# Decoder layer in float32r pairs: one list of weight splits for the whole layer, and VectorE's transposes tied behind it

## The chip, the core and the metric

One core of a Trainium2 chip (trn2) runs one launch. The metric is the device time of an execution in microseconds (us). The engines named below are TensorE (PE in the profile, with PEld for its weight loads), VectorE (DVE), ScalarE (ACT), GpSimd (POOL) and SyncE (SP), which issues most DMAs.

## The reference, cut to what matters

One decoder layer on 256 tokens, 2048 channels, everything in float32:

```
h    = rmsnorm(x);  proj = h @ w_in          # 2048 x 13312: glu, q, k, v, q_xa, three gates
conv = conformer(glu) ; da = diff_attention(q, k, v) ; xa = cross_attention(q_xa, rmsnorm(mem) @ w_mem_kv)
merged = g0 * (conv @ w_conv_out) + g1 * (da @ w_da_out) + g2 * (xa @ w_xa_out)
x = x + merged @ w_mix_out
x = x + square(relu(rmsnorm(x) @ w_up)) @ w_down      # 2048 -> 8192 -> 2048
return rmsnorm(x)
```

The products with the weights are nearly all of the work, and each weight is used once.

## The kernel before

**How a product is made.** float32 is split into two float32r parts: hi, a rounded copy, and lo, the rest. A product is then three matmuls: hi x whi, hi x wlo, lo x whi. `group` (L297) makes one block of 512 columns for all 256 tokens: over k in steps of two k tiles (a *block*, 256 rows of a weight), it loads raw (512 KB, SyncE's queue, L319), lets ScalarE write whi (L327) and VectorE wlo = raw - whi (L328), and runs 12 matmuls (2 k tiles, 2 token tiles, 3 products, L309 to L311) into two PSUM banks. A group over 2048 rows has eight blocks, over 1024 rows four. There are 560 blocks. Tiles rotate: raw has 5 buffers, whi 4, wlo 3. After the last block, `evac` hands the result on.

**The groups in order.** w_in for the convolution (4 groups), w_mem_kv (4), w_in for q_xa, q, k, v (8). Then, four times, three gate groups (w_in) and one group each of w_xa_out, w_da_out, w_conv_out, whose gated sum is a chunk `mg`. Then four groups of w_mix_out, whose results are added to x (tiles x1, L892). Then four times (j): four groups of w_up, each giving a chunk `ru`, and four of w_down (L933 adds to x1).

**Transposes.** The stationary operand of a product must be an activation with features on the partitions. Chunks mg, x1 and ru have tokens there, so `to_parts_dve` (L265) turns a chunk of 512 features with VectorE's 32 x 32 transposes: `block_transpose2` (L253, for mg, ru, and also kx and xq) takes 16 instructions of 32x256, `block_transpose` (L241, for x1, which lies in one tile for each token tile) 32 instructions of 32x128. Then two conversions follow, each of hi by ScalarE and of lo by VectorE (L272 to L284).

**What sets the order.** Such work is a generator in a `Task` (L78), put in a lane by `spawn` (L128). After each block of matmuls `side_step` (L137) ticks the task at the head of each lane: one step up to its next `yield`, at rate 1. A group whose activation is not finished calls `finish` on its task before the matmuls that need it (L333). So a chunk's task is spread over the blocks of the next group in the program. [...] `later` (L143) adds an edge of order alone: the first instruction is not put before the second.

Of the kernel before, what the change touches and what calls it, by code (L numbers as in the profile page):

```python
# [10 lines left out]
F32 = mybir.dt.float32  # L11
F32R = mybir.dt.float32r
I32 = mybir.dt.int32
U32 = mybir.dt.uint32
AF = mybir.ActivationFunctionType
# [4 lines left out]
P = 128  # L20
# [12 lines left out]
WARM = 8  # L33
LAMBDA_INIT = 0.8 - 0.6
# [4 lines left out]
def _turn_pieces(n):  # L39
    """1/(2 pi) cut into n float32 pieces of 12 bits each."""  # L40
    digits = "0.15915494309189533576888376337251436203445964574045644874766734405889679763"
    from fractions import Fraction

    rest = Fraction(digits)
    out = []
    for i in range(n):
        ulp = Fraction(1, 2 ** (14 + 12 * i))
        q = rest // ulp
        out.append(float(q * ulp))
        rest -= q * ulp  # L50
    return out


class Act:
    """An activation, transposed: [feature, token] as two float32r parts whose sum is the float32 value."""
# [22 lines left out]
class Task:  # L78
    def __init__(self, gen, rate=1.0):
        self.gen = gen  # L80
        self.rate = rate
        self.credit = 0.0
        self.done = False
# [20 lines left out]
def decoder_layer_kernel(  # L104
# [18 lines left out]
    # ---------------------------------------------------------------- side work  # L123
# [4 lines left out]
    def spawn(gen, lane="t", rate=1.0):  # L128
        t = Task(gen, rate)
        lanes[lane].append(t)  # L130
        return t
# [11 lines left out]
    def later(ins, first):  # L143
        """Keeps work that nothing else holds back from being issued before `first`."""
        tc.add_manual_dep(
            ins.ins, first.ins.name,
            mybir.DependencyInfo(mybir.DependencyClass.NoSync, mybir.DependencyReason.DATA),
            reason="issue order",
        )
# [6 lines left out]
    # ---------------------------------------------------------------- constants  # L156
# [3 lines left out]
    with tc.high_priority():  # L160
        nc.vector.memset(neg_half, -0.5)
        nc.vector.memset(ones, 1.0 / CH)
        make_identity(nc, ident)
        # the tensor engine's clock rises only under load
        pw = psum.tile([P, P], F32, tag="at", name="pw")
        for _ in range(WARM):
            nc.tensor.matmul(pw, ones, ones, start=True, stop=True)
        warm = const.tile([P, 1], F32, name="warm")
        nc.scalar.activation(warm, neg_half[:, 0:1], AF.Square)
# [26 lines left out]
    # ---------------------------------------------------------------- pieces  # L196
    def rsqrt_of(ss, n, dim, name):
        """(ss / dim + eps) ** -0.5 for a [P, n] of sums of squares."""
        m = const.tile([P, n], F32, name=name + "_m")
        nc.vector.tensor_scalar(m, ss, 1.0 / dim, EPS, ALU.mult, ALU.add)  # L200
        rv = const.tile([P, n], F32, name=name)
        nc.gpsimd.tensor_tensor(rv, m, neg_half[:, :n], op=ALU.pow)
        return rv
# [14 lines left out]
    def to_parts(src, dst, kt0, nkt, gname=None):  # L218
        """src [tok, NT, nkt * P] -> the transposed parts of dst from k tile kt0."""
        for b in range(0, nkt, 2):  # L220
            ps = psum.tile([P, 2, S], F32, tag="tr", name="tr")
            for c in range(2):
                for t in range(NT):
                    transpose(ps[:, c, t * P : (t + 1) * P], src[t][:, (b + c) * P : (b + c + 1) * P])
            yield
            k = kt0 + b
            if gname is None:
                nc.scalar.copy(dst.hi(k, 2), ps)
                nc.vector.tensor_tensor(dst.lo(k, 2), ps, dst.hi(k, 2).bitcast(F32), op=ALU.subtract)
            else:  # L230
                for c in range(2):
                    g = vcol(gname, k + c)
                    nc.scalar.activation(dst.hi(k + c), ps[:, c : c + 1, :], AF.Copy, scale=g)  # L233
                for c in range(2):
                    g = vcol(gname, k + c)
                    nc.vector.scalar_tensor_tensor(
                        dst.lo(k + c), ps[:, c : c + 1, :], g, dst.hi(k + c).bitcast(F32), ALU.mult, ALU.subtract
                    )
            yield

    def block_transpose(src, dst):  # L241
        """src, one [tok, G] for each token tile -> dst [feature, G // P, tok], by 32 x 32 blocks on the vector engine."""
        B = 32
        for q in range(P // B):
            for c in range(P // B):
                for t in range(NT):
                    nc.vector.transpose(  # L247
                        dst[c * B : (c + 1) * B, :, t * P + q * B : t * P + (q + 1) * B],
                        src[t].rearrange("p (j c k) -> p j c k", c=P // B, k=B)[q * B : (q + 1) * B, :, c, :],
                    )  # L250
            yield

    def block_transpose2(src, dst):  # L253
        """As block_transpose, of one [tok, NT, G] tile."""
# [3 lines left out]
        for q in range(P // B):  # L258
            for c in range(P // B):
                nc.vector.transpose(  # L260
                    out_v[c * B : (c + 1) * B, :, :, q * B : (q + 1) * B], in_v[q * B : (q + 1) * B, :, :, c, :]
                )
            yield

    def to_parts_dve(src, dst, kt0, gname=None):  # L265
        """src [tok, NT, G], or a list by token tile -> the transposed parts of dst from k tile kt0."""
        st = work.tile([P, G // P, S], F32, tag="chunk", name="st", bufs=4)
        yield from (block_transpose if isinstance(src, list) else block_transpose2)(src, st)
# [17 lines left out]
    def transpose_plain(src, dst, kt0, nkt):  # L286
        """src [tok, NT, nkt * P] -> dst [feature, kt, tok], float32."""
# [8 lines left out]

    def group(w, r0, c0, act, evac, prep=None, split=0):  # L297
        """psum[t] = act^T [tok, K] @ w[r0 : r0 + K, c0 : c0 + G], each handed to evac(t, psum).

        The last `split` blocks of k run token tile by token tile."""  # L300
# [12 lines left out]
        held = []  # L313
        for kb in range(nkb):
            k = kb * KB
            if prep is not None:
                prep(k)
            raw = wpool.tile([P, KB, G], F32, tag="raw", name="raw", bufs=5)
            ld = nc.sync.dma_start(  # L319
                raw, w[r0 + k * P : r0 + (k + KB) * P, c0 : c0 + G].rearrange("(c p) n -> p c n", p=P)  # L320
            )
            if prep is not None and kb < 2:
                later(ld, first_load[kb])
            whi = wpool.tile([P, KB, G], F32R, tag="whi", name="whi", bufs=4)
            wlo = wpool.tile([P, KB, G], F32R, tag="wlo", name="wlo")
            with tc.high_priority():
                nc.scalar.copy(whi, raw)  # L327
                nc.vector.tensor_tensor(wlo, raw, whi.bitcast(F32), op=ALU.subtract)  # L328
# [39 lines left out]
    # ---------------------------------------------------------------- normed x  # L368
# [17 lines left out]
    # rotary tables, taps, lambda  # L386
# [69 lines left out]
    # ---------------------------------------------------------------- convolution branch  # L456
# [137 lines left out]
    # ---------------------------------------------------------------- memory: keys and values  # L594
# [26 lines left out]
    # ---------------------------------------------------------------- cross attention  # L621
# [67 lines left out]
    # ---------------------------------------------------------------- differential attention  # L689
# [140 lines left out]
    # ---------------------------------------------------------------- gated merge  # L830
# [12 lines left out]
    def products(c):  # L843
# [14 lines left out]
        tk = spawn(to_parts_dve(mg, mT, c * 4))  # L858
# [7 lines left out]
    # ---------------------------------------------------------------- output projection, residual  # L866
    x1 = [units.tile([P, D], F32, tag="unit", name=f"x1_{t}") for t in range(NT)]
    for t in range(NT):
        later(nc.gpsimd.dma_start(x1[t], x[t * P : (t + 1) * P, :]), mark[0])
# [6 lines left out]
    def squares(src, dst, c):  # L876
        for t in range(NT):
            junk = work.tile([P, G], F32, tag="t2k", name="junk", bufs=4)
            nc.scalar.activation(junk, src[t][:, c * G : (c + 1) * G], AF.Square, accum_out=dst[:, t, c : c + 1])

    def x1_task(c):
        yield from to_parts_dve([x1[t][:, c * G : (c + 1) * G] for t in range(NT)], x1T, c * 4, "g_mlp")
        squares(x1, ss1, c)
# [4 lines left out]
    for c in range(NC4):  # L888
        def f(ps, c=c):
            for t in range(NT):  # L890
                xs = x1[t][:, c * G : (c + 1) * G]
                nc.vector.tensor_tensor(xs, ps[t], xs, op=ALU.add)  # L892
            tk = spawn(x1_task(c))
# [3 lines left out]
    # ---------------------------------------------------------------- feed forward  # L897
    ss2 = const.tile([P, NT, 8], F32, name="ss2")

    def final_scale(t):  # L900
# [3 lines left out]
        for c in range(NC4):  # L904
            xs = x1[t][:, c * G : (c + 1) * G]
# [8 lines left out]
    for j in range(DFF // D):  # L914
        uu = Act(units, f"ff{j}", 16)
        for g in range(4):
            def f(ps, g=g, uu=uu):
# [5 lines left out]
                tk = spawn(to_parts_dve(ru, uu, g * 4))  # L923
                uu.tasks[g * 4 : g * 4 + 4] = [tk] * 4
            group(w_up, 0, j * D + g * G, x1T, both(f))
        for c in range(NC4):
# [3 lines left out]
            def f(t, ps, c=c, last=last):  # L930
                xs = x1[t][:, c * G : (c + 1) * G]
# [42 lines left out]
```

## Time and profile before

| | |
|---|---|
| measured, median of 3 runs | 1622.68 us (1622.25 to 1623.86) |
| profiled execution, span from first to last instruction | 1620.9 us (the profile gives no time of that execution beyond its span) |
| TensorE busy | 1585.9 us, 98% |
| VectorE busy | 1135.4 us, 70% |
| ScalarE busy | 782.5 us, 48% |
| DMA | 304.79 MB, mean 188 GB/s |
| chain of waits that ended last | TensorE 84%, VectorE 13% |

How to read it: the kernel is one stream of matmuls with short interruptions. A busy share is a mean over all stages. Where TensorE is idle, the rows of its waits say what it waited for, and the order of VectorE's and ScalarE's instructions around that moment says why it came late.

### The profile page before, as it was taken

The page shows a single profiled execution, that of the slowest core. Times are in us where ns is not written, and L with a number is a line of the kernel's source. Part 1 is how long each engine was busy: PE and PEld are TensorE (multiplying, and loading weights), DVE is VectorE, ACT ScalarE, POOL GpSimd, SP SyncE. Part 2 cuts the span into 40 slices and gives each one's busy share as a digit, 9 for nine tenths or more (in the row PEclk, how much of TensorE's full clock was granted, in tenths as well). Part 3 has the DMA queues.
Part 4 walks back from the last instruction along what each step waited for, and adds up shares of the span by engine and source line. Part 5 has one row for each costly group of instructions (what it writes and reads, how often), then busy time and mean ns, then how long its engine had stood idle before and what let it go on. Part 6 is the DMA issues. An engine that isn't in the chain of part 4 may idle for free.

```text
span 1620.9 us, 19587 instructions
## 1 busy us (share of the span) xinstructions
PE 1585.9 (98%) x7020; PEld 1301.2 (80%) x7020; DVE 1135.4 (70%) x1705; ACT 782.5 (48%) x1006; POOL 20.5 (1%) x33
## 2 busy tenths in 40 slices
PE   8999999999999999999999999999999999999997
PEld 7888788888888888888877787887888878887786
DVE  5589989888877456474689877457765676548754
ACT  6554444455784444444344544335543454344543
POOL 1000000010000000000000000000000000000000
PEclk9999999999999999999999999999999999999999
DMA  8665665556556666667655565665656656665563
GB/s 265 199 220 163 193 187 171 160 157 192 158 170 188 199 190 191 194 191 219 239 183 168 170 207 182 195 194 160 203 192 197 183 166 208 194 193 179 167 211 125
DMA packets 156934, 304.79 MB, mean 188 GB/s; under 512 B 9578, under 2 KB 10164, under 8 KB 156452
## 3 DMA queue, kind: packets, MB, share of 16 engines
q1 hardware_dynamic: 156036, 299.96, 60.3%
q0 software_dynamic: 768, 3.57, 0.7%
q8 instruction: 55, 0.90, 0.2%
q14 instruction: 43, 0.35, 0.1%
q10 hardware_dynamic: 32, 0.01, 0.0%
HBM read 301.40 MB, written 2.10 MB: 187 GB/s over the span
## 4 chain that ended last, share of the span: by engine, by line
PE 84%; DVE 13%; issue 2%; DMA 0%; DVEq 0%; ACT 0%; SPq 0%; POOLq 0%; POOL 0%
PE acc L310 28%; PE acc L311 27%; PE acc L309 27%; DVE st L260 6%; DVE wlo L328 4%; DVE st L247 2%; PE tr L173 1%; PE xs L642 0%; PE xo L675 0%; DMA raw<-in_w_in_dram 0%; PE ds L737 0%; DVE kxT L260 0%; PE do L788 0%; DVE conv L487 0%; DVEq L328 0%
## 5 line engine op out<-in xcount | busy, mean ns | idle before, releaser
L328 DVE TENSOR_TENSOR wlo<-raw,whi 128x1024 fp32r<-128x1024 f32 x560 | 682.4, 1224 | 402.8 <-PE acc L310 341.6
L327 ACT CAST whi<-raw 128x1024 fp32r<-128x1024 f32 x560 | 591.1, 1056 | 707.3 <-PE acc L311 671.9
L310 PE MATMUL acc<-wlo,xT_hi 128*128 128x512 f32 x768 | 302.2, 394 | 1.5 <-DVE wlo L328 1.5
L311 PE MATMUL acc<-whi,xT_lo 128*128 128x512 f32 x768 | 299.6, 393 | 0.0
L309 PE MATMUL acc<-whi,xT_hi 128*128 128x512 f32 x768 | 294.0, 395 | 3.0 <-ACT xT_hi L233 3.0
L310 PE MATMUL acc<-wlo,x1T_hi 128*128 128x512 f32 x512 | 200.7, 392 | 11.8 <-DVE wlo L328 11.7
L310 PE MATMUL acc<-wlo,ff_hi 128*128 128x512 f32 x512 | 199.7, 390 | 3.5 <-DVE wlo L328 3.5
L311 PE MATMUL acc<-whi,ff_lo 128*128 128x512 f32 x512 | 199.3, 389 | 0.0
L311 PE MATMUL acc<-whi,x1T_lo 128*128 128x512 f32 x512 | 199.2, 390 | 0.0
L309 PE MATMUL acc<-whi,ff_hi 128*128 128x512 f32 x512 | 193.2, 389 | 0.0
L309 PE MATMUL acc<-whi,x1T_hi 128*128 128x512 f32 x512 | 186.2, 389 | 0.0
L310 PEld LDWEIGHTS acc<-wlo,xT_hi 128*128 128x128 f32 x768 | 144.6, 189 | 32.9 <-DVE wlo L328 3.5
L309 PEld LDWEIGHTS acc<-whi,xT_hi 128*128 128x128 f32 x768 | 144.3, 189 | 32.8 <-ACT xT_hi L233 3.2
L311 PEld LDWEIGHTS acc<-whi,xT_lo 128*128 128x128 f32 x768 | 144.7, 189 | 29.9
L310 PEld LDWEIGHTS acc<-wlo,x1T_hi 128*128 128x128 f32 x512 | 96.1, 188 | 37.5 <-DVE wlo L328 17.7
L310 PEld LDWEIGHTS acc<-wlo,ff_hi 128*128 128x128 f32 x512 | 96.1, 188 | 25.2 <-DVE wlo L328 5.2
L260 DVE STREAM_TRANSPOSE st<-ru 32x256 f32<-32x256 f32 x256 | 111.4, 435 | 3.3
L309 PEld LDWEIGHTS acc<-whi,x1T_hi 128*128 128x128 f32 x512 | 96.1, 188 | 20.1
L309 PEld LDWEIGHTS acc<-whi,ff_hi 128*128 128x128 f32 x512 | 96.1, 188 | 19.9
L311 PEld LDWEIGHTS acc<-whi,ff_lo 128*128 128x128 f32 x512 | 96.1, 188 | 19.8
L311 PEld LDWEIGHTS acc<-whi,x1T_lo 128*128 128x128 f32 x512 | 96.1, 188 | 19.6
L487 DVE SCALAR_TENSOR_TENSOR conv<-uT,taps,conv 128x255 f32<-128x255 f32 (+29 forms) x240 | 98.2, 468 | 0.1
(208 smaller groups left out, 1400.2 us busy)
## 6 DMA issues: line engine op xcount, KB each, us to landing
raw<-in_w_in_dram SPq DMA_DIRECT2D x192, 512.0 KB, 4.3
raw<-in_w_up_dram SPq DMA_DIRECT2D x128, 512.0 KB, 3.9
raw<-in_w_down_dram SPq DMA_DIRECT2D x128, 512.0 KB, 4.8
raw<-in_w_mem_kv_dram SPq DMA_DIRECT2D x32, 512.0 KB, 4.1
raw<-in_w_mix_out_dram SPq DMA_DIRECT2D x32, 512.0 KB, 4.5
raw<-in_w_xa_out_dram SPq DMA_DIRECT2D x16, 512.0 KB, 4.2
raw<-in_w_da_out_dram SPq DMA_DIRECT2D x16, 512.0 KB, 4.7
raw<-in_w_conv_out_dram SPq DMA_DIRECT2D x16, 512.0 KB, 4.6
```

Source lines behind the costliest of these rows:

```text
L173: nc.tensor.transpose(dst, src, ident[:k, :k])
L247: nc.vector.transpose(dst[c * B : (c + 1) * B, :, t * P + q * B : t * P + (q + 1) * B], src[t].rearrange("p (j c k) -> p j c k", c=P // B, ...
L260: nc.vector.transpose(out_v[c * B : (c + 1) * B, :, :, q * B : (q + 1) * B], in_v[q * B : (q + 1) * B, :, :, c, :])
L309: nc.tensor.matmul(ps[t], hi[:, tt], whi[:, c, :], start=kt == 0, stop=False)
L310: nc.tensor.matmul(ps[t], hi[:, tt], wlo[:, c, :], start=False, stop=False)
L311: return nc.tensor.matmul(ps[t], lo[:, tt], whi[:, c, :], start=False, stop=kt == nkt - 1)
L327: nc.scalar.copy(whi, raw)
L328: nc.vector.tensor_tensor(wlo, raw, whi.bitcast(F32), op=ALU.subtract)
L487: ins = nc.vector.scalar_tensor_tensor(conv[:, cb, d:], uT[:, cb, : S - d], w, conv[:, cb, d:], ALU.mult, ALU.add)
```

## The change

- All blocks of all groups stand in one list in the program's order (`plan_groups`). `produce` takes the next one: raw's DMA, whi, wlo. `group` calls it up to twice in a block while at most AHEAD = 3 splits are ready, and takes the oldest. So a split is issued three blocks ahead, across group boundaries. The first group, with its own loads of x, takes them one by one.
- wlo has 4 buffers for 3, raw 4 for 5; whi stays at 4.
- `lo_mark` is the newest wlo issued. Each instruction of `block_transpose2` gets an edge of order behind it. As a step of the task issues four transposes, they lie in fours behind successive wlo.
- `hold`: the tasks of mg, x1 and ru skip their first tick.
- x1 changes from two tiles [P, 2048], one for each token tile, to two tiles [P, 2, NT, 512], so that a chunk of 512 columns has both token tiles side by side. `block_transpose` goes; x1 uses `block_transpose2`. The load of x becomes four DMAs for two.
- Comments and docstrings go.

```
-    def __init__(self, gen, rate=1.0):
+    def __init__(self, gen, rate=1.0, hold=0):
-        self.credit = 0.0
+        self.credit = -float(hold) * rate
...
     def block_transpose2(src, dst):
...
         for q in range(P // B):
             for c in range(P // B):
-                nc.vector.transpose(
+                ins = nc.vector.transpose(
                     out_v[c * B : (c + 1) * B, :, :, q * B : (q + 1) * B], in_v[q * B : (q + 1) * B, :, :, c, :]
                 )
+                later(ins, lo_mark[0])
             yield
...
+    def produce(after=None):
+        job = next(stream, None)
+        if job is None:
+            return
+        w, r0, c0, kb = job
+        r = r0 + kb * KB * P
+        raw = wpool.tile([P, KB, G], F32, tag="raw", name="raw", bufs=4)
+        ld = nc.sync.dma_start(raw, w[r : r + KB * P, c0 : c0 + G].rearrange("(c p) n -> p c n", p=P))
+        if after is not None:
+            later(ld, after)
+        whi = wpool.tile([P, KB, G], F32R, tag="whi", name="whi", bufs=WB)
+        wlo = wpool.tile([P, KB, G], F32R, tag="wlo", name="wlo", bufs=WB)
+        with tc.high_priority():
+            nc.scalar.copy(whi, raw)
+            lo_mark[0] = nc.vector.tensor_tensor(wlo, raw, whi.bitcast(F32), op=ALU.subtract)
+        ready.append((whi, wlo))
...
             if prep is not None:
                 prep(k)
-            raw = wpool.tile([P, KB, G], F32, tag="raw", name="raw", bufs=5)
...
+                if kb < 2:
+                    produce(first_load[kb])
+            else:
+                for _ in range(2):
+                    if len(ready) <= AHEAD:
+                        produce()
+            whi, wlo = ready.pop(0) if ready else produce_now()
...
-        tk = spawn(to_parts_dve(mg, mT, c * 4))
+        tk = spawn(to_parts_dve(mg, mT, c * 4), hold=HOLD)
...
-    x1 = [units.tile([P, D], F32, tag="unit", name=f"x1_{t}") for t in range(NT)]
-    for t in range(NT):
-        later(nc.gpsimd.dma_start(x1[t], x[t * P : (t + 1) * P, :]), mark[0])
+    x1u = [units.tile([P, 2, NT, G], F32, tag="unit", name=f"x1_{u}") for u in range(NC4 // 2)]
+    x1c = [x1u[c // 2][:, c % 2] for c in range(NC4)]
+    for c in range(NC4):
+        later(
+            nc.gpsimd.dma_start(x1c[c], x[:, c * G : (c + 1) * G].rearrange("(t p) n -> p t n", p=P)), mark[0]
+        )
...
     def x1_task(c):
-        yield from to_parts_dve([x1[t][:, c * G : (c + 1) * G] for t in range(NT)], x1T, c * 4, "g_mlp")
-        squares(x1, ss1, c)
+        yield from to_parts_dve(x1c[c], x1T, c * 4, "g_mlp")
+        for t in range(NT):
+            junk = work.tile([P, G], F32, tag="t2k", name="junk", bufs=4)
+            nc.scalar.activation(junk, x1c[c][:, t, :], AF.Square, accum_out=ss1[:, t, c : c + 1])
...
-            tk = spawn(x1_task(c))
+            tk = spawn(x1_task(c), hold=HOLD)
...
-                tk = spawn(to_parts_dve(ru, uu, g * 4))
+                tk = spawn(to_parts_dve(ru, uu, g * 4), hold=HOLD)
```

## Rows read from the trace of the kernel before

**Rows 1.** The page's first lines: span, busy time and instructions of each engine.
```profile
span 1620.9 us, 19587 instructions
...
PE 1585.9 (98%) x7020; PEld 1301.2 (80%) x7020; DVE 1135.4 (70%) x1705; ACT 782.5 (48%) x1006; POOL 20.5 (1%) x33
```

**Rows 2.** Waits of TensorE: us in total, times, longest us.
```profile
PE acc L310 <- DVE wlo L328: 21.8, 27, 1.1
```

**Rows 3.** Instructions of TensorE by tile: busy, mean ns | idle before, releaser.
```profile
L310 PE MATMUL acc<-wlo,xT_hi 128*128 128x512 f32 x768 | 302.2, 394 | 1.5 <-DVE wlo L328 1.5
...
L310 PE MATMUL acc<-wlo,x1T_hi 128*128 128x512 f32 x512 | 200.7, 392 | 11.8 <-DVE wlo L328 11.7
L310 PE MATMUL acc<-wlo,ff_hi 128*128 128x512 f32 x512 | 199.7, 390 | 3.5 <-DVE wlo L328 3.5
...
L310 PE MATMUL acc<-wlo,memT_hi 128*128 128x512 f32 x128 | 51.3, 401 | 1.2 <-DVE wlo L328 1.2
L310 PE MATMUL acc<-wlo,mT_hi 128*128 128x512 f32 x128 | 50.5, 395 | 4.3 <-DVE wlo L328 3.9
```

**Rows 4.** Timeline of TensorE, one w_up group: start, us, instruction [idle before].
```profile
1153.40 0.39 PE L309 MATMUL acc<-whi,x1T_hi 128*128 128x512 f32 x1
...
1153.86 0.39 PE L311 MATMUL acc<-whi,x1T_lo 128*128 128x512 f32 x1
...
1155.58 0.50 PE L310 MATMUL acc<-wlo,x1T_hi 128*128 128x512 f32 x1 [0.88 <-DVE wlo L328]
```

**Rows 5.** Timeline of VectorE, the same group.
```profile
1145.95 1.22 DVE L328 TENSOR_TENSOR wlo<-raw,whi 128x1024 fp32r<-128x1024 f32 x1 [1.04 <-PE acc L310]
1147.10 7.17 DVE L260 STREAM_TRANSPOSE st<-ru 32x256 f32<-32x256 f32 x16
1154.29 2.36 DVE L328 TENSOR_TENSOR wlo<-raw,whi 128x1024 fp32r<-128x1024 f32 x2
1156.57 0.69 DVE L273 TENSOR_TENSOR ff_lo<-st,ff_hi 128x512 fp32r<-128x512 f32 x1
```

**Rows 6.** Timeline of ScalarE, the same group.
```profile
1148.84 1.06 ACT L327 CAST whi<-raw 128x1024 fp32r<-128x1024 f32 x1 [1.36 <-PE acc L311]
1151.56 1.06 ACT L327 CAST whi<-raw 128x1024 fp32r<-128x1024 f32 x1 [1.66 <-PE acc L311]
1154.30 1.14 ACT L272 CAST ff_hi<-st 128x512 fp32r<-128x512 f32 x2 [1.68 <-DVE st L260]
```

**Rows 7.** Instructions of VectorE by line: the transposes.
```profile
L260 DVE STREAM_TRANSPOSE st<-ru 32x256 f32<-32x256 f32 x256 | 111.4, 435 | 3.3
...
L247 DVE STREAM_TRANSPOSE st<-x 32x128 f32<-32x128 f32 x128 | 37.3, 298 | 1.5
```

**Rows 8.** Stretches: length, then each engine's busy time, granted clock, DMA share, GB/s.
```profile
122.00:202.00 80.00, 78.78 (x344) 62.96 (x344) 78.41 (x165) 37.73 (x44) 0.00 (x0) 1.00 0.59 179
6.00:9.00 3.00, 0.09 (x1) 0.00 (x0) 0.30 (x1) 2.22 (x7) 0.00 (x0) 0.79 1.03 366
9.00:12.00 3.00, 2.91 (x7) 2.13 (x8) 3.00 (x6) 2.97 (x8) 0.00 (x0) 0.50 1.05 390
12.00:14.40 2.40, 2.40 (x7) 1.73 (x6) 1.60 (x2) 1.39 (x3) 0.00 (x0) 0.50 1.05 386
906.00:909.00 3.00, 1.86 (x9) 1.33 (x8) 2.90 (x9) 0.90 (x1) 0.00 (x0) 1.00 0.20 31
```

**Rows 9.** Instructions of ScalarE by line: x1T's hi.
```profile
L276 ACT ACTIVATE x1T_hi<-st,vec 128x256 fp32r<-128x256 f32 x16 | 6.9, 501 | 9.5 <-DVE st L247 9.5
```

**Rows 10.** Instructions on tile x: ns min/median/max, first and last start.
```profile
L892 DVE TENSOR_TENSOR x<-acc,x x8: 685/689/692, 823.9 to 896.5; 128x512 f32<-128x512 f32 x8
...
L869 POOL DMA_DIRECT2D x<-in_x_dram x2: 553/570/588, 758.3 to 769.0; - x2
```

**Rows 11.** Waits of SyncE's queue.
```profile
SPq L319 <- DVE wlo L328: 1147.3, 470, 7.9
```

**Rows 12.** DMA issues: KB each, median us to landing.
```profile
raw<-in_w_down_dram SPq DMA_DIRECT2D x128, 512.0 KB, 4.8
```

More of the change, by code (lines that the diff above doesn't have):

```diff
@@ L33 @@
 WARM = 8
+WB = 4
+AHEAD = 3
+HOLD = 1
 LAMBDA_INIT = 0.8 - 0.6
@@ L126, in decoder_layer_kernel, with spawn @@
     lanes = {"t": [], "conv": [], "a0": [], "a1": []}
-    def spawn(gen, lane="t", rate=1.0):
-        t = Task(gen, rate)
+    def spawn(gen, lane="t", rate=1.0, hold=0):
+        t = Task(gen, rate, hold)
         lanes[lane].append(t)
@@ L239, in to_parts @@
             yield
[L241 to L245, printed above, removed]
-                for t in range(NT):
-                    nc.vector.transpose(
[L248 to L251, printed above, removed]
     def block_transpose2(src, dst):
@@ L259, in block_transpose2 @@
             for c in range(P // B):
-                nc.vector.transpose(
+                ins = nc.vector.transpose(
                     out_v[c * B : (c + 1) * B, :, :, q * B : (q + 1) * B], in_v[q * B : (q + 1) * B, :, :, c, :]
                 )
+                later(ins, lo_mark[0])
             yield
@@ L267, in to_parts_dve @@
         st = work.tile([P, G // P, S], F32, tag="chunk", name="st", bufs=4)
-        yield from (block_transpose if isinstance(src, list) else block_transpose2)(src, st)
+        yield from block_transpose2(src, st)
         for b in range(0, G // P, 2):
@@ L295, in transpose_plain, with plan_groups, add, produce_now @@
             yield
+    plan = []
+    def plan_groups():
+        def add(w, c0, rows=D, r0=0):
+            plan.append((w, r0, c0, rows // P // KB))
+        for c0 in (CH, 0, CH + G, G):
+            add(w_in, c0)
+        for g in range(4):
+            add(w_mem_kv, g * G)
+        for c0 in (5120, 2048, 3072, 4096):
+            add(w_in, c0)
+            add(w_in, c0 + G)
+        for c in range(D // G):
+            for i in range(3):
+                add(w_in, 6144 + i * D + c * G)
+            for w in (w_xa_out, w_da_out, w_conv_out):
+                add(w, c * G, CH)
+        for c in range(D // G):
+            add(w_mix_out, c * G)
+        for j in range(DFF // D):
+            for g in range(4):
+                add(w_up, j * D + g * G)
+            for c in range(D // G):
+                add(w_down, c * G, D, j * D)
+    plan_groups()
+    at = [0]
+    stream = ((w, r0, c0, kb) for w, r0, c0, nkb in plan for kb in range(nkb))
+    ready = []
+    lo_mark = [None]
+    def produce(after=None):
[14 more added lines that the diff above has]
+        ready.append((whi, wlo))
+    def produce_now():
+        produce()
+        return ready.pop(0)
     def group(w, r0, c0, act, evac, prep=None, split=0):
@@ L313, in group @@
         held = []
+        assert plan[at[0]] == (w, r0, c0, nkb)
+        at[0] += 1
         for kb in range(nkb):
@@ L317, in group @@
                 prep(k)
-            raw = wpool.tile([P, KB, G], F32, tag="raw", name="raw", bufs=5)
[L319 to L328, printed above, removed]
+                if kb < 2:
[3 more added lines that the diff above has]
+                    if len(ready) <= AHEAD:
+                        produce()
+            whi, wlo = ready.pop(0) if ready else produce_now()
             if kb >= nkb - split:
@@ L864, in decoder_layer_kernel @@
         products(c)
-    x1 = [units.tile([P, D], F32, tag="unit", name=f"x1_{t}") for t in range(NT)]
-    for t in range(NT):
-        later(nc.gpsimd.dma_start(x1[t], x[t * P : (t + 1) * P, :]), mark[0])
+    x1u = [units.tile([P, 2, NT, G], F32, tag="unit", name=f"x1_{u}") for u in range(NC4 // 2)]
[4 more added lines that the diff above has]
+        )
     gfin = units.tile([P, D], F32, tag="unit", name="gfin")
@@ L874, in decoder_layer_kernel, with x1_task @@
     ss1 = const.tile([P, NT, 4], F32, name="ss1")
-    def squares(src, dst, c):
+    def x1_task(c):
+        yield from to_parts_dve(x1c[c], x1T, c * 4, "g_mlp")
         for t in range(NT):
             junk = work.tile([P, G], F32, tag="t2k", name="junk", bufs=4)
-            nc.scalar.activation(junk, src[t][:, c * G : (c + 1) * G], AF.Square, accum_out=dst[:, t, c : c + 1])
-    def x1_task(c):
-        yield from to_parts_dve([x1[t][:, c * G : (c + 1) * G] for t in range(NT)], x1T, c * 4, "g_mlp")
-        squares(x1, ss1, c)
+            nc.scalar.activation(junk, x1c[c][:, t, :], AF.Square, accum_out=ss1[:, t, c : c + 1])
         if c == NC4 - 1:
@@ L890, in f @@
             for t in range(NT):
-                xs = x1[t][:, c * G : (c + 1) * G]
+                xs = x1c[c][:, t, :]
                 nc.vector.tensor_tensor(xs, ps[t], xs, op=ALU.add)
-            tk = spawn(x1_task(c))
+            tk = spawn(x1_task(c), hold=HOLD)
             x1T.tasks[c * 4 : c * 4 + 4] = [tk] * 4
@@ L904, in final_scale @@
         for c in range(NC4):
-            xs = x1[t][:, c * G : (c + 1) * G]
+            xs = x1c[c][:, t, :]
             if c == NC4 - 1:
@@ L930, in f @@
             def f(t, ps, c=c, last=last):
-                xs = x1[t][:, c * G : (c + 1) * G]
+                xs = x1c[c][:, t, :]
                 if not last:
```

## The prediction

> **What bounds the kernel now.** I read the page's first part, then TensorE's waits, then the same waits by tile, then the order on the two engines that feed it. TensorE is busy for 1585.9 of a span of 1620.9 us [rows 1], so all that better feeding can give lies in the 35 us between. Among TensorE's waits only one kind repeats: a product with wlo, L310, waits for VectorE's wlo, 27 times, 21.8 us [rows 2]. By tile its idle time is 1.5 (xT), 11.8 (x1T), 3.5 (ff), 1.2 (memT) and 4.3 us (mT) [rows 3], 22.3 in all; what is left of the 35 is the start and the tail, which the change does not touch.
>
> One such wait in full: matmuls start 0.23 us apart (1153.40, 1153.86 two later), while one's own record is 0.39; the product at 1155.58 comes after 0.88 idle [rows 4]. A block (two k tiles) is 12 matmuls and needs one whi and one wlo; undisturbed, whi follow each other by 2.72 us (1148.84, 1151.56) [rows 6], so a matmul takes 2.72 / 12 = 0.227. One that starts from idle also loses the 0.39 - 0.227 = 0.16 by which neighbours overlap. Beside it VectorE ran 16 transposes in one go, 7.17 us from 1147.10, and only at 1154.29 the next two wlo [rows 5]. Three wlo buffers hold at most three blocks of supply, and 7.2 us of transposes use it up. [...]
>
> **The change part by part.** The measured median, 1622.68, is 1.78 above the profiled span; I keep those 1.78 fixed and sum against the span.
>
> *Taken away: the waits for wlo.* The idle time is 22.3 and 27 restarts cost 27 x 0.16 = 4.3: 26.6 us. Will they go? With the split three blocks ahead and four buffers, wlo of block k+3 may start when block k-1 has left TensorE: 0.16 for the last product's end, 1.06 for whi [rows 6], 1.18 for wlo (2.36 for two [rows 5]): done 2.4 us into block k, and needed 3 x 2.72 = 8.16 after its start, 5.8 to spare. Where transposes run, VectorE has 1.18 + 7.17/4 = 2.97 us of work in a block of 2.72: it falls back 0.25 a block, about 1 us over four. The spare covers that, and a group of eight blocks holds 8 x 1.18 + 7.17 + 1.38 (two ff_lo of 0.69 [rows 5]) = 18.0 of 21.8 us. So every wait on wlo in the x1T, ff and mT groups should go. The memT stretch is different: VectorE is busy 78.41 of 80 us there [rows 8], and one block more of supply does not lighten it. Its waits are 1.2 + 4 x 0.16 = 1.8 us; between all and none of it I keep half, 0.9.
>
> *Added: transposes in fours, each four behind the newest wlo, first four one block late (hold).* Cost on the path: nothing while another group's blocks stand between producing and using a tile, which is so for 3 of 4 of the mT chunks and of the ff chunks. The chunk that is made last before its consumer starts is late. Call B6 the start of block 6, which needs it. The fours are issued in blocks 1 to 4, behind wlo of blocks 4 to 7. The first ends 2.4 + 1.8 = 4.2 us into block 1; with 0.25 lost at each later one, the fourth ends 4.2 + 0.75 = 4.95 into block 4, 0.5 before B6. ff_hi is 0.57 (1.14 for two [rows 6]): B6 + 0.1. On VectorE wlo of block 8 goes first, as the two wlo do in [rows 5]: until B6 + 0.7, then ff_lo 0.69: B6 + 1.4. The third product wants ff_lo at B6 + 0.1 + 0.45: 0.85 late, 0.95 in all; were ff_lo to go ahead of wlo, 0.35. The trace of before has no such wait, so its bounds are 0 (the order fills it with the next group's blocks) and 0.95; I take 0.8, near the row's order. There are five: mT into w_mix_out, and ff into w_down four times: 4.0 us.
>
> *The same for x1T, the sixth hand-off.* Its task has nine ticks, with the hold, for eight blocks in a group (four transposes, two conversions, the squares, the end, the hold), and only the head of the lane ticks. So each chunk starts later than the one before: the second one in block 1, the third in block 2, the last in block 3 of the first w_up group. At block 6 two of its fours are not yet issued, and they come behind wlo of block 9, which waits for block 5 to end. With two fours before it: wlo of block 9 done B6 + 2.9, eight transposes 3.6, x1T_hi 0.5 [rows 9]: B6 + 7.0. [...] I take 3.0.
>
> [...]
>
> *Block shape of x1.* A chunk now takes 16 transposes of 0.435 instead of 32 of 0.298 [rows 7]: 7.0 for 9.5 us, 2.6 less VectorE work in each of four chunks. It lies beside TensorE; it is part of why the mT waits go, and has no term of its own. The load of x, now four DMAs of shorter rows, is issued at 769.0 and first used at 823.9 [rows 10]: nothing.
>
> *raw from 5 to 4 buffers, wlo from 3 to 4.* SP's loads wait on wlo (1147.3 us in total [rows 11]), so a load goes out when wlo of four blocks earlier is done: 4 x 2.72 = 10.9 us to the next wlo of that buffer, less 4.8 landing [rows 12], 1.06 and 1.18: 3.8 us spare. Cost nothing; it begins to cost where landings pass 8.6 us.
>
> **Sum.** 1620.9 - 26.6 + 0.9 + 4.0 + 3.0 = 1602.2 of span, with 1.78 outside it 1604.0 us.
>
> **The rivals.**
> *Clean:* the order fills all six hand-offs and the memT waits go: 1622.7 - 26.6 = 1596.1. For it: TensorE was already given blocks out of order across groups, and 5.8 us of spare is much. [...]
> *Hand-offs at their dear end:* x1T's gap 7.0 with the clock's 2.7, five hand-offs at 1.4 (0.95 and half a microsecond of further lag), the memT waits stay (1.8): 1596.1 + 9.7 + 7.0 + 1.8 = 1614.6. For it: nothing has been seen that fills the gaps; against: two buffered blocks are there to run.
> *It does not do what it says:* the engine's order still puts wlo last before the product, since VectorE has 2.97 us per block against 2.72; the 27 waits shrink a little and come back as many small ones: about 1622. Against: 18.0 of 21.8 us per group.
> *Slower:* transposes behind a wlo that itself waits for TensorE make a ring: product, wlo, transposes, product. [...] It decides from 26.6 / 6 = 4.4 us per hand-off upward. For it: the x1T tasks do fall behind by a tick per group; against: an ff task has 7 ticks and 1 of hold, just the eight of a group.
>
> **How the numbers follow.** The forecast, 1604 with its own range of 1599 to 1609, has 0.40; clean 0.28; the dear end 0.18; no gain 0.06; slower 0.08. A measurement of this kernel can tell 0.2%, 3.2 us. The first three are all faster by more: 0.86; the same 0.06; slower 0.08. The range goes from just below clean to the dear end, 1595 to 1615, and leaves out the last two and a little of the ends.
>
> **What would show it.** Right: TensorE's waits for wlo under 3 us; transposes in fours between wlo; TensorE's largest new wait one on x1T_hi or st in the first w_up group, of about 3 us, and five of under 1 us on ff or mT parts at the start of w_mix_out and w_down. Wrong: a wait on wlo that stays near 0.88 at every w_up group (the tie does not spread them), gaps of 4 us and more at the five hand-offs, whi waiting for raw's DMA, or a granted clock under 1.00 after 20 us.

## The result, and the profile after

The changed kernel takes 1595.0 us (1594.6 to 1595.3, four runs) against 1623.3: the ratio is 0.983, with an interval of 0.981 to 0.984. 1604 was forecast, with 1595 to 1615 around it, so the time lies on the lower edge of that range and outside the forecast's own 1599 to 1609; the rival "clean" had put it at 1596.1.

The first lines of the changed kernel's page, beside [rows 1]:

```profile
span 1593.4 us, 19128 instructions
...
PE 1577.7 (99%) x7020; PEld 1304.3 (82%) x7020; DVE 1131.0 (71%) x1641; ACT 781.1 (49%) x1006; POOL 23.3 (1%) x35
```

The span is 27.5 us shorter, and TensorE's busy time only 8.2: the other 19.3 were idle time. Its waits, as in [rows 2] (us in total, times, longest us), with L356 to L358 for the former L309 to L311 and L337 for L328:

```profile
PE acc L357 <- DVE wlo L337: 1.2, 2, 0.8
PE acc L356 <- ACT x1T_hi L268: 1.1, 1, 1.1
```

27 waits for wlo, 21.8 us, have become two, 1.2 us. One new wait has come, for x1T_hi. The waits in [rows 3] of memT, x1T, ff and mT products for wlo are all gone; both that are left belong to products with xT, at 202 and 206 us.

VectorE's timeline in a w_up group (start, us, instruction, idle before it), which answers to [rows 5]:

```profile
1130.64 1.23 DVE L337 TENSOR_TENSOR wlo<-raw,whi 128x1024 fp32r<-128x1024 f32 x1 [1.45 <-ACT whi L336]
1131.78 1.78 DVE L251 STREAM_TRANSPOSE st<-ru 32x256 f32<-32x256 f32 x4
1133.59 1.23 DVE L337 TENSOR_TENSOR wlo<-raw,whi 128x1024 fp32r<-128x1024 f32 x1
...
1142.82 1.22 DVE L337 TENSOR_TENSOR wlo<-raw,whi 128x1024 fp32r<-128x1024 f32 x1
1143.96 1.28 DVE L265 TENSOR_TENSOR ff_lo<-st,ff_hi 128x512 fp32r<-128x512 f32 x2
```

The transposes stand in fours of 1.78 us, and a wlo starts about every 3 us, where [rows 5] had 7.17 us of transposes without one. The step "2.97 us of VectorE work in a block" is seen as written: 1130.64, 1133.59.

The one new wait, TensorE's timeline at the first w_up group:

```profile
907.37 0.61 PE L356 MATMUL acc<-whi,x1T_hi 128*128 128x512 f32 x2
909.13 0.50 PE L356 MATMUL acc<-whi,x1T_hi 128*128 128x512 f32 x1 [1.15 <-ACT x1T_hi L268]
909.47 0.39 PE L357 MATMUL acc<-wlo,x1T_hi 128*128 128x512 f32 x1
```

x1T_hi is 1.15 us late, not 3.0. The granted clock is 1.00 over 905 to 912 us, so the gap cost its own length and no clock. The start from idle costs more than the 0.16 of the forecast: the matmul at 909.13 is followed by the next 0.34 later. It was so before, too; 0.34 us behind the product of [rows 4] stands, on the same timeline:

```profile
1155.92 0.40 PE L311 MATMUL acc<-whi,x1T_lo 128*128 128x512 f32 x1
```

So a restart takes 0.16 (the overlap of the forecast) + (0.34 - 0.227) = 0.27 us beyond the idle time. The same sum, taken at each of the 27 waits for wlo before and at the three waits here, gives 0.27 or 0.28.

How the gain divides: for each pair of matmuls that follow each other, take the time from start to start less 0.227. From the first w_mix_out product on (801.6 us before, 798.2 after), this excess sums to 27.5 us before and 2.7 after; ahead of it, to 16.8 and 12.2. That is 24.8 + 4.6 = 29.4 gained. Waits of the products and their restarts are 26.0 of it (29.2 before, 3.2 after); the other 3.4 are slips that no row calls a wait. These matmuls start 0.7 later, the tail is 0.4 longer and the stretches of TensorE's other work 0.7: 27.6, against 27.5 measured.

### The profile page after: what moved, and what is told of

It reads as the page before. It is cut to its first block, busy times and chain, and to the rows that moved or that the text cites. A ratio compares the mean times of both kernels' runs of the same rounds, so it can differ in the third digit from the quotient of the medians.

```text
span 1593.4 us, 19128 instructions
## 1 busy us (share of the span) xinstructions
PE 1577.7 (99%) x7020; PEld 1304.3 (82%) x7020; DVE 1131.0 (71%) x1641; ACT 781.1 (49%) x1006; POOL 23.3 (1%) x35
## 4 chain that ended last, share of the span: by engine, by line
PE 96%; DVE 3%; issue 1%; DMA 0%; ACT 0%; SPq 0%; POOLq 0%; POOL 0%; DVEq 0%; ACTq 0%
PE acc L356 31%; PE acc L357 31%; PE acc L358 31%; DVE wlo L337 1%; DVE kxT L251 1%; PE tr L176 1%; DVE conv L532 0%; PE xs L687 0%; PE xo L720 0%; DVE st L251 0%; DMA raw<-in_w_in_dram 0%; PE ds L782 0%; PE do L833 0%; ACT whi L336 0%; PE xpt L176 0%
## 5 line engine op out<-in xcount | busy, mean ns | idle before, releaser
L337 DVE TENSOR_TENSOR wlo<-raw,whi 128x1024 fp32r<-128x1024 f32 x560 | 684.6, 1224 | 423.6 <-ACT whi L336 419.9
L356 PE MATMUL acc<-whi,xT_hi 128*128 128x512 f32 x768 | 299.9, 396 | 3.3 <-ACT xT_hi L236 3.3
L358 PE MATMUL acc<-whi,xT_lo 128*128 128x512 f32 x768 | 299.7, 393 | 0.0
L356 PE MATMUL acc<-whi,x1T_hi 128*128 128x512 f32 x512 | 198.2, 389 | 1.1 <-ACT x1T_hi L268 1.1
L356 PE MATMUL acc<-whi,ff_hi 128*128 128x512 f32 x512 | 198.7, 390 | 0.0
L358 PE MATMUL acc<-whi,x1T_lo 128*128 128x512 f32 x512 | 198.4, 389 | 0.0
L358 PE MATMUL acc<-whi,ff_lo 128*128 128x512 f32 x512 | 197.9, 389 | 0.0
L356 PEld LDWEIGHTS acc<-whi,xT_hi 128*128 128x128 f32 x768 | 144.5, 189 | 33.0 <-ACT xT_hi L236 3.5
L358 PEld LDWEIGHTS acc<-whi,xT_lo 128*128 128x128 f32 x768 | 144.8, 189 | 30.1
L356 PEld LDWEIGHTS acc<-whi,x1T_hi 128*128 128x128 f32 x512 | 96.1, 188 | 21.5 <-ACT x1T_hi L268 1.6
L356 PEld LDWEIGHTS acc<-whi,ff_hi 128*128 128x128 f32 x512 | 96.1, 188 | 21.2 <-ACT ff_hi L264 1.4
L358 PEld LDWEIGHTS acc<-whi,ff_lo 128*128 128x128 f32 x512 | 96.1, 188 | 20.1
L358 PEld LDWEIGHTS acc<-whi,x1T_lo 128*128 128x128 f32 x512 | 96.1, 188 | 20.0
```

The source lines that it names most:

```text
L337: lo_mark[0] = nc.vector.tensor_tensor(wlo, raw, whi.bitcast(F32), op=ALU.subtract)
L356: nc.tensor.matmul(ps[t], hi[:, tt], whi[:, c, :], start=kt == 0, stop=False)
L358: return nc.tensor.matmul(ps[t], lo[:, tt], whi[:, c, :], start=False, stop=kt == nkt - 1)
```

## The experiments

The theory of the forecast was that two parts remove the waits together: supply (the list and the fourth wlo) and the tie, and that the tie is paid for at the hand-offs. The rivals were that one of them does it alone, and that the hand-offs cost nothing.

**Without the tie.**

```
             for c in range(P // B):
                 ins = nc.vector.transpose(...)
-                later(ins, lo_mark[0])
```

> The changed kernel without the edge that ties transposes behind the newest wlo; four wlo buffers, the list and the split three ahead stay. Theory T (spreading in fours is needed): the 16 transposes stand together again, begin about 3.2 us into the first block, last 7.2, so wlo of block 4 is done about 11.6 where block 4 starts at 10.9: a wait on wlo of 0.3 to 0.8 us at each of some 20 groups, 6 to 16 us in all, time 1601 to 1611. Rival B (one more buffer is enough): no waits on wlo in the mT, x1T and ff groups, time 1594 to 1596.

Measured: 1590.5 us, ratio 0.981 (0.979 to 0.982). VectorE's timeline in a w_up group, and TensorE's waits:

```profile
1147.28 6.27 DVE L251 STREAM_TRANSPOSE st<-ru 32x256 f32<-32x256 f32 x14 [0.40 <-ACT ru L966]
1153.58 1.23 DVE L336 TENSOR_TENSOR wlo<-raw,whi 128x1024 fp32r<-128x1024 f32 x1
1154.84 0.90 DVE L251 STREAM_TRANSPOSE st<-ru 32x256 f32<-32x256 f32 x2
```

```profile
PE acc L356 <- DVE wlo L336: 0.2, 1, 0.2
```

14 transposes run together again, 6.27 us, almost as in [rows 5], and the wlo behind them comes as late; but TensorE waits for wlo 0.2 us in all. So the tie isn't what removes the waits here: one block more in store is 2.72 us more, and the longest wait was 1.1. The wait for x1T_hi is gone with the tie.

**The tie with three wlo buffers.**

```
-AHEAD = 3
+AHEAD = 2
...
-        wlo = wpool.tile(..., name="wlo", bufs=WB)
+        wlo = wpool.tile(..., name="wlo", bufs=3)
```

> The changed kernel with three wlo buffers as before and the split two blocks ahead instead of three; the tie stays. Theory T: wlo is done 2.4 us into a block and needed after 5.4; the lag of 1 us over four fours leaves 2 us, so no wait on wlo at the w_up groups, time 1594 to 1598. Rival B (the fourth buffer carries the gain): the waits of about 0.9 us come back at the groups with transposes, time 1605 to 1620.

Measured: 1596.8 us, ratio 0.985 (0.983 to 0.986). TensorE's waits for wlo:

```profile
PE acc L357 <- DVE wlo L337: 5.9, 5, 1.8
```

Three of the five lie at 196 to 204 us, where VectorE is full (busy for 14.66 of 15 us from 190 to 205), two at the start of w_up (904 and 909 us, 3.1 us), where theory T had none. The w_up and w_down groups behind them have none. So the tie does remove most of the waits when it has to.

**One buffer alone, in the kernel before.**

```
-            raw = wpool.tile([P, KB, G], F32, tag="raw", name="raw", bufs=5)
+            raw = wpool.tile([P, KB, G], F32, tag="raw", name="raw", bufs=4)
...
-            wlo = wpool.tile([P, KB, G], F32R, tag="wlo", name="wlo")
+            wlo = wpool.tile([P, KB, G], F32R, tag="wlo", name="wlo", bufs=4)
```

> The kernel before with wlo 4 and raw 4 buffers and nothing else. Theory T: the transposes still stand 16 (mg, ru) or more (x1) together; most waits on wlo stay but shorter by up to a part of the 2.7 us that a block gives; time 1600 to 1615. Rival B: nearly the whole gain, time 1594 to 1598.

Measured: 1594.0 us, ratio 0.983 (0.981 to 0.984). TensorE's waits for wlo:

```profile
PE acc L310 <- DVE wlo L328: 1.8, 5, 0.6
```

Without list, tie, hold and the new x1 tiles, a raw buffer traded for a wlo buffer gives the whole gain of the change. Of the 1.8 us left, 0.2 lie at 169 us beside memT, and 1.5 in four waits at 852 to 921 us, beside the 32 small transposes of each x1 chunk. They were 1.1 us each before, so there the additional buffer shortened the waits and didn't end them.

**Neither, with the rest of the change.**

```
-AHEAD = 3
+AHEAD = 2
...
-                later(ins, lo_mark[0])
...
-        wlo = wpool.tile(..., name="wlo", bufs=WB)
+        wlo = wpool.tile(..., name="wlo", bufs=3)
```

> The list and the new shape of x1, but neither the tie nor the fourth wlo buffer (split two blocks ahead). The last corner of tie by buffer. Theory 2 (either of the two suffices, and the rest of the change gives next to nothing): waits on wlo of 0.9 us idle at the mT, x1T and ff groups as before, some 20 of them; x1's shape takes a part off those of the w_mix_out groups; time 1612 to 1620. Rival (list or shape carry part of the gain): 1595 to 1608.

Measured: 1619.3 us, ratio 0.998 (0.997 to 0.999). The waits are back, in the number of [rows 2]:

```profile
PE acc L356 <- DVE wlo L336: 20.4, 27, 0.9
```

So the list over all groups, the hold and the new x1 tiles give some 4 us (2 to 5) of 28 by themselves. By the sums from start to start 2.8 us of it lie at the four x1 chunks, where the waits of 1.14 us became 0.7. raw has four buffers here as well, so the gain of the trade is wlo's fourth buffer. With the two parts taken apart (medians, us):

| | three wlo buffers | four |
|---|---|---|
| no tie | 1619.3 | 1590.5, 1591.3 |
| tie | 1596.8 | 1595.0, 1594.8 |

Either part removes most of the waits. Together they aren't better than the fourth buffer alone: the tie on top costs. The second numbers of the right column come from a repeat of both on one chip:

> The changed kernel once more, beside the next three on the same chip, so that the cost of the tie is read from runs of one sitting. Theory K (the tie costs): 1594 to 1596, 3 to 5 us above the kernel without the tie. Rival: the difference came from the sitting, and the two are equal within 1.5 us.

> The changed kernel without the tie, once more in the same sitting. Theory K: 1590 to 1592, 3 to 5 us under the changed kernel. Rival: as the changed kernel.

1594.8 (1594.5 to 1595.1) with the tie, 1591.3 (1590.3 to 1592.3) without: 3.5 us.

**Where the tie costs: the hold, and the early transposes.** First, no hold (`HOLD = 0` for 1) with the tie kept:

> The changed kernel with HOLD = 0: the chunks' tasks start in the first block. Theory N (nine ticks for eight blocks make the x1T gap): without the hold an x1 task has eight ticks, none falls behind, the wait of 1.1 us on x1T_hi in the first w_up group goes; time 1593.0 to 1594.5. Rival: the hold keeps transposes from colliding with the additions into x1, so waits on wlo appear at groups that start with them; time 1596 or more.

Measured: 1592.5 us, ratio 0.981 (0.980 to 0.982). TensorE's wait for x1T_hi is gone, the two for wlo at 202 and 206 us stay (1.2 us). The time is half a microsecond under theory N's range, because the five hand-offs, which cost 0.23 us each in the changed kernel, cost nothing here either. Then the tie kept for mg, x1 and ru alone, not for kx and xq:

```
-                later(ins, lo_mark[0])
+                if tie:
+                    later(ins, lo_mark[0])
...
-        yield from block_transpose2(src, st)
+        yield from block_transpose2(src, st, tie=True)
```

> The changed kernel with the tie on the transposes of mg, x1 and ru alone; those of kx and xq are free. Theory K (the tie costs where VectorE is full, in the memT stretch): the two waits on wlo around 202 to 206 us, 1.2 us idle and 1.6 with the restarts, go, the x1T one stays; time 1592.5 to 1594. Rival: these waits come from the list or from raw's four buffers, and stay; time 1595.

Measured: 1594.0 us, ratio 0.982 (0.981 to 0.983). Here it is the other way round:

```profile
PE acc L357 <- ACT x1T_hi L269: 1.2, 1, 1.2
...
PE acc L358 <- DVE wlo L338: 0.2, 1, 0.2
```

Why the tie hurts at 202 us is on VectorE's timeline of the changed kernel:

```profile
201.24 1.22 DVE L337 TENSOR_TENSOR wlo<-raw,whi 128x1024 fp32r<-128x1024 f32 x1
202.49 1.80 DVE L251 STREAM_TRANSPOSE kxT<-kx 32x256 f32<-32x256 f32 x4
204.32 0.83 DVE L532 SCALAR_TENSOR_TENSOR conv<-uT,taps,conv 128x232 f32<-128x232 f32 x2
205.07 1.22 DVE L337 TENSOR_TENSOR wlo<-raw,whi 128x1024 fp32r<-128x1024 f32 x1
```

The engine has no idle time there. A four of kx transposes, tied behind the wlo of 201.24, goes ahead of convolution work and of the wlo of 205.07, for which TensorE waits 0.81 us. By the sums from start to start the tie's cost divides so: the gap at x1T 1.55 and five hand-offs of 0.23, 2.7 us, which go without the hold (2.5 measured); and 0.8 net here, where two waits and restarts of 1.8 stand against a wait of 0.2 at 169 us and slips that the run without the tie has (1.0 measured with kx and xq free). That is 3.5, as measured.

The hold matters only with the tie; without both:

> The changed kernel with neither tie nor hold. Theory: without the tie a late start costs nothing (the order ran no x1T gap), so the hold is neutral: 1590 to 1592. Rival: without the hold the transposes meet the additions into x1 and waits on wlo return: 1593 or more.

1591.2 us, ratio 0.980 (0.979 to 0.982), the same as without the tie alone. And the list, without the tie, called for one block at a time (`AHEAD = 0`):

> The run without the tie, and AHEAD = 0 as well: each split is issued in the program where it is used, as before, not three blocks earlier. [...] Rival A (the list is worth something): 1593 to 1596.

1591.1 us, ratio 0.980 (0.979 to 0.982): below rival A's 1593, and as the run without the tie (1590.5, 1591.3). So splitting three blocks ahead in the program gives nothing that can be measured. These versions without the tie are faster than both kernels.

**Why the hand-offs cost so little.** In TensorE's order of the changed kernel, 26 matmuls of the second w_up group (blocks 8 and 9 and two of block 10) stand ahead of the first product that needs the last chunk of x1T: 98 matmuls with x1T have started by then, where the order in the next run, which keeps the groups apart, has 72. 26 x 0.227 is 5.9 us, where the forecast, with 3.0 left of 7.0, had 4. To test that this filling is what makes the hand-offs cheap, it was forbidden: from the second w_mix_out group on, the first products of a group come behind the last matmul of the group before (`mark[0]`).

```
-            nc.tensor.matmul(ps[t], hi[:, tt], whi[:, c, :], start=kt == 0, stop=False)
+            mm0 = nc.tensor.matmul(ps[t], hi[:, tt], whi[:, c, :], start=kt == 0, stop=False)
+            if kt == 0 and behind is not None:
+                later(mm0, behind)
...
+        behind = mark[0] if at[0] > 40 else None
```

> The changed kernel, with an edge of order that keeps the first matmuls of each group from w_mix_out's second on behind the last matmul of the group before: TensorE's order can no longer fill a late hand-off with the next group's blocks. Theory F (the order's filling is why my hand-offs cost nothing): TensorE waits about 7 us on x1T_hi at block 6 of the first w_up group, and 0.4 to 1.0 us at each of five hand-offs into w_mix_out and w_down; time 1602 to 1607, the higher if the clock falls after the 7 us gap. Rival E (the transposed tiles came early enough by themselves): no new waits but the 1.1 us one, time 1594 to 1596.

Measured: 1605.8 us, ratio 0.990 (0.989 to 0.991). TensorE's waits:

```profile
PE acc L356 <- ACT x1T_hi L268: 7.1, 1, 7.1
...
PE acc L356 <- ACT ff_hi L264: 1.5, 4, 0.4
...
PE acc L356 <- ACT mT_hi L264: 0.4, 1, 0.4
```

With nothing to fill in, x1T_hi is 7.15 us late (the forecast reckoned 7.0 and took 3.0). VectorE's timeline has the two fours together that the forecast put behind the wlo of block 9:

```profile
903.83 1.22 DVE L337 TENSOR_TENSOR wlo<-raw,whi 128x1024 fp32r<-128x1024 f32 x1
905.08 3.59 DVE L251 STREAM_TRANSPOSE st<-x 32x256 f32<-32x256 f32 x8
```

At the five hand-offs ff_hi or mT_hi is 0.37 us late, and ff_lo or mT_lo comes late as well, since wlo goes ahead of it on VectorE. The second hand-off into w_down, TensorE and then VectorE:

```profile
1173.41 0.50 PE L356 MATMUL acc<-whi,ff_hi 128*128 128x512 f32 x1 [0.37 <-ACT ff_hi L264]
...
1174.62 0.73 PE L360 MATMUL acc<-whi,ff_lo 128*128 128x512 f32 x2
```

```profile
1172.74 1.23 DVE L337 TENSOR_TENSOR wlo<-raw,whi 128x1024 fp32r<-128x1024 f32 x1
1173.88 1.29 DVE L265 TENSOR_TENSOR ff_lo<-st,ff_hi 128x512 fp32r<-128x512 f32 x2
```

From start to start each of the five costs 0.97 us above the pace, 0.64 with the wait and its restart and the rest at the ff_lo or mT_lo products. The forecast's dear end was 0.95, of which it gave 0.1 to ff_hi and the rest to ff_lo. So lateness was reckoned well at x1T, and at the five in sum though not in its parts, and the filling was put too low. At x1T 7.0 - 5.9 = 1.1, and 1.15 was measured.

The stretches around this gap (columns as in [rows 8]; the figure behind POOL's is the granted clock as a share of the full one):

```profile
905.00:909.00 4.00, 0.00 (x0) 0.00 (x0) 3.54 (x9) 0.30 (x1) 0.00 (x0) 0.55 0.48 138
909.00:911.00 2.00, 1.73 (x4) 1.45 (x5) 1.69 (x4) 1.42 (x4) 0.00 (x0) 0.50 0.00 0
...
913.00:916.00 3.00, 3.00 (x15) 2.44 (x13) 1.17 (x1) 1.05 (x1) 0.00 (x0) 1.00 0.01 3
```

and TensorE's timeline in them:

```profile
909.27 0.80 PE L356 MATMUL acc<-whi,x1T_hi 128*128 128x512 f32 x1 [7.15 <-ACT x1T_hi L268]
...
911.99 0.52 PE L356 MATMUL acc<-whi,x1T_hi 128*128 128x512 f32 x1
912.35 0.39 PE L359 MATMUL acc<-wlo,x1T_hi 128*128 128x512 f32 x1
```

The engine stood still from 902.1 to 909.3; the clock fell to 0.50 and was back after matmuls from 909.3 to about 912.0, where the record of a matmul goes from 0.52 back to 0.39. After the 1.15 us of the changed kernel the clock stayed at 1.00. The price here is half of 2.7 us, 1.4, where the forecast's dear end had 2.7. The gap with its clock costs 8.8 us from start to start, for 1.55 in the changed kernel, and the five hand-offs 0.97 each for 0.23: 11.0 more, where this kernel's span is 10.3 longer. The 0.7 between are not assigned.

**One raw buffer less again** (`bufs=3` for 4):

> The changed kernel with three raw buffers instead of four. By my sum of the spare time: 3 x 2.72 = 8.2 from one split to the next of that buffer, less 4.6 landing, 1.06 whi and 1.18 wlo leaves 1.3 us, so loads start to matter only where VectorE lags by 1 us: 1595 to 1602. Rival (loads bind already with four, and the spare is not there): waits on raw's DMA in every group, 1610 or more.

Measured: 1605.6 us, ratio 0.989 (0.988 to 0.991), between what the two expected. TensorE's waits, and ScalarE's for raw:

```profile
PE acc L356 <- ACT ff_hi L264: 2.4, 1, 2.4
PE acc L356 <- ACT whi L336: 2.1, 1, 2.1
PE acc L357 <- DVE wlo L337: 2.0, 3, 0.8
PE acc L356 <- ACT mT_hi L264: 1.2, 1, 1.2
```

```profile
ACT whi L336 <- DMA raw<-in_w_in_dram: 39.7, 23, 3.1
```

raw's DMA now reaches TensorE, once through whi (2.1 us), and elsewhere through late whi, late wlo and the transposes tied behind them (ff_hi, 2.4 us): for the blocks of w_in alone ScalarE waits 23 times, 39.7 us, where the changed kernel has 13.2 us in 6 waits. The two longest gaps cost more than their length:

```profile
1000.05 0.50 PE L356 MATMUL acc<-whi,ff_hi 128*128 128x512 f32 x1 [2.35 <-ACT ff_hi L264]
```

```profile
1000.00:1001.00 1.00, 0.95 (x4) 0.82 (x5) 1.00 (x2) 1.00 (x2) 0.00 (x0) 1.00 0.52 197
1002.00:1004.00 2.00, 2.00 (x6) 1.58 (x5) 0.94 (x1) 0.00 (x0) 0.00 (x0) 0.50 0.82 241
1005.00:1006.00 1.00, 1.00 (x6) 0.83 (x5) 0.00 (x0) 0.85 (x1) 0.00 (x0) 1.00 0.85 287
```

After 2.35 us of standstill matmuls ran at 1.00 until about 1001.6 us, then at 0.50 until about 1005, which cost 1.6 us; behind the gap of 2.1 us that ended at 34.2 us the same happened from about 35.6 to 39.0 us, for another 1.6. In the run of the tie with three wlo buffers a wait of 1.84 us, at 909 us, left the clock at 1.00 (the mean over that run is 0.998, here 0.994). Of the 10.4 us by which this kernel's span is longer, waits and restarts are 5.2 and the clock 3.2. With three buffers a load goes out 2.72 us later against its use, so the 3.8 us to spare become 1.1, and that is used up. At four raw cost TensorE nothing, as the forecast said, but it wasn't far from it.

## Why the prediction was right, and 9 us high

By its own steps:

- *What bounds the kernel.* Right: 19.3 us of idle time went, nearly all at waits for wlo.
- *Taken away, 26.6.* The place and the idle time were right (21.8 in the waits; the 22.3 of [rows 3] has shorter gaps in it), the restarts mis-sized: 0.27 instead of 0.16 makes 27 x 0.27 = 7.3 and 29.2 in all. The overlap of one record was taken for the whole loss; the matmul behind the slow one starts late, too, and [rows 4] ended one row too early to show it.
- *memT keeps half, 0.9.* These waits went (there were three, the forecast counted four); two others came just behind that stretch, at 202 and 206 us, from the tie itself: 1.2 + 2 x 0.27 = 1.7.
- *x1T hand-off, 3.0.* **This step failed in its size:** the late time of 7.0 was right (7.15 when unfilled), but the order fills 5.9 us of it, not 4. 1.15 + 0.27 = 1.4 is left. The 4, by which the forecast came from 7.0 to its 3.0, was the author's estimate, and no run shows it. Why [rows 5] has 16 in one go stays open.
- *Five hand-offs, 4.0.* **So did this one, for the same reason.** They take 0.23 each, 1.1 in all. Unfilled they cost 0.97, with wlo ahead of ff_lo as the forecast had it, so its 0.8 was near the price without filling. In the changed kernel the order puts two matmuls of the next group ahead of the late ff_hi products and ten more ahead of the late ff_lo ones.

TensorE's timeline where w_up hands over to w_down for the second time, and ScalarE's conversion of the late chunk beside it:

```profile
1164.71 1.04 PE L356 MATMUL acc<-whi,ff_hi 128*128 128x512 f32 x3
1165.59 0.39 PE L357 MATMUL acc<-wlo,ff_hi 128*128 128x512 f32 x1
1165.82 0.40 PE L356 MATMUL acc<-whi,ff_hi 128*128 128x512 f32 x1
```

```profile
1164.58 1.14 ACT L264 CAST ff_hi<-st 128x512 fp32r<-128x512 f32 x2 [1.33 <-DVE st L251]
```

The first half of ff_hi is done at 1164.58 + 0.57 = 1165.15. Three matmuls from 1164.71 on, the first two of them of the next group, take 0.88 to the next start, 0.2 more than at the pace, and that is the whole price.

- *The clock* had no share, as in the sum: behind the gap of 1.15 us it was 1.00. With the gap that the forecast expected, 3.0, it would most likely have had one, by an estimate from the other runs: it was 0.50 behind gaps of 2.1 and 2.35 us (three raw buffers), at 1.6 us each, and at the one of 7.15 us (groups kept apart), at 1.4. The 2.7 of the dear end, half of the 5.4 us at 0.50 in [rows 8], is shown by no run; 1.4 to 1.6 was measured in its place. That the sum has no term for the clock did no harm because the gap was 1.15.
- *raw and x1's shape at nothing.* raw holds. x1's shape was not tried by itself; in the four-wlo kernel before, the waits beside the 32 small transposes of x1 (1.5 us) are the ones that the changed kernel doesn't have.
- *What removes the waits.* The forecast gave it to the list, the buffer and the tie together. Either of the last two suffices for most of it. Its step "it falls back 0.25 a block" needed the tie; that a spare of 5.8 us comes close to 6.3 us of transposes in one go without any tie, it did not ask.

Corrected: 1620.9 - 29.2 + 1.7 + 1.4 + 1.1 + 1.8 (later start, tail, other work) = 1597.7, against a span of 1593.4. The 4.3 us between are slips of under 0.3 us each from the pace of 0.227, which no row calls a wait and which became fewer; five of them, 1.3 us, were of 0.2 to 0.3 us, four of these at the x1 chunks. What made the rest isn't shown. These slips had no term in the forecast, so even with every step at its measured size it would have been 4 us high. The 8.8 us by which 1602.2 was too high are then 2.6 for the restarts, 2.9 for the hand-offs, 1.6 for x1T and 4.3 for the slips, less 0.8 at memT and 1.8 for start, tail and other work. That the stated range held the time owes to its lower bound, which was set by the rival "clean"; that rival's number is nearest, but it had all hand-offs filled without a rest and no slips. The rival "slower" had its ring: transposes behind wlo do delay x1T by 7 us, but once and not at all six hand-offs, and filled. "It does not do what it says" is refuted by the fours in the timeline.

## What to carry to other kernels

When an engine waits in short stalls for a producer that is busy with a long run of something else, compare the longest stall with one more buffer's worth of work: here 1.1 against 2.72 us, and one buffer gave all that an order of its own gave. The comparison is no proof: beside the 32 small transposes of the x1 chunks waits of 1.1 us became 0.2 to 0.6 and did not go. An order edge that fixes this tightly may cost (here 3.5 us, 0.8 of it where the producer had no idle time), so after adding the buffer, take the edge away and look. And a hand-off was late only by what the consumer's order did not fill, here 1.15 of 7.15 us; count the independent instructions that stand ahead of the late one before pricing it.

## What of the hardware was not expected

A matmul that started after a stall cost 0.27 us beyond the stall, at the 27 waits for wlo of the kernel before as at the three waits of the changed one. With three raw buffers the granted clock was 0.50 behind gaps of 2.1 and 2.35 us, but only after matmuls had run again at 1.00 for over a microsecond (from 34.2 to about 35.6 us, and from 1000.05 to about 1001.6); behind 1.15 us (the changed kernel) and 1.84 us (three wlo buffers) it stayed at 1.00. And the clock came back faster than at the kernel's start: after the 7.15 us of standstill, with the groups kept apart, it was at 1.00 again after 2.7 us of matmuls, while at the start of the kernel before it was 0.50 for the 5.4 us from 9.0 to 14.4 [rows 8].
